# Orders at three stage changes, w_ada a place ahead, and early splits moved off Pool

## The chip, the cores and the metric

One core of a Trainium2 chip runs the whole block in one launch. The metric is device time in microseconds, the median of the runs shown.

## The reference

One transformer-like block in float32 on x of 1024 tokens by 1024 channels:

```
mod = silu(c) @ w_ada + b_ada            # 6 x 1024 columns: shift, scale, gate, twice
h  = rmsnorm(x) * (1 + scale_m) + shift_m
z  = h @ w_in                            # q, k, v, forget logits, pool, conv, 3 x 1024 gate logits
y  = sum over 3 branches of sigmoid(gate) * (branch @ w_branch part)
x  = x + gate_m * rmsnorm(y @ w_out)
h2 = rmsnorm(x) * (1 + scale_f) + shift_f
out = x + gate_f * rmsnorm(relu(h2 @ w_ff1)**2 @ w_ff2)
```

The branches are causal attention with forget gates (8 heads), causal pooling means, and a gated short convolution.

## The kernel before, in words

Every large product is made of three float32r matmuls: each operand is split into a high part (a copy rounded to float32r, `hi`) and a low part (`lo` = operand - hi), and hi·hi, hi·lo and lo·hi are summed in PSUM. A split is two instructions: `split` (L112) and `fsplit` (L686) put the copy on ACT and the subtraction on DVE; `pool_split` (L117) puts both on Pool (GpSimd); `early_split` (L126) the copy on ACT, ahead of its turn, and the subtraction on Pool; `mixed_split` (L121) the copy on Pool and the subtraction on DVE.

The work goes in stages on one core, from memory through SBUF:

1. Start (L137 to L390). x comes in halves of four token tiles. `norm_half` (L258) squares each on ACT, makes 1/rms and scales each tile; the string `XE` (L34) says for each of eight tiles which engine scales it (G Pool, A ACT, V DVE). Column by column k, two 128x1024 tiles of w_ada are loaded on SP's queue and reduced against silu(c) by one DVE instruction each (`ada`, L229), `am` (L317) is made from them, the tile is transposed on TensorE, ACT makes `h` and the high part of `hT`, DVE the low part (L288). w_va (128x264 per k, L322) is split on Pool; three weight tiles of the conv branch (`U_LOADS`, L312) are loaded and split there too. The raw buffers of w_va are two.
2. q, k, v, attention, pooling and conv, with projections woven in (to about 410 us).
3. Gates. Four gate tiles by plain projection (`gate`, L607: sigmoid on ACT, then a store through Pool's queue to DRAM), then ten pairs of gate tiles in a seven-product scheme (`gate_pair`, L807), for which the four `hT` quadrants are combined to `G1` to `G4` first (L764 to L793), each split by `fsplit`. In the pairs, `more_ada` (L617) is called four times a pair: it loads one more w_ada tile and reduces it at once. These tiles, raw weights and sums share eight buffers, tag `M`. After pair 8, `mod_rows` makes the rows for the later norms.
4. Branch projections and merge; then the output projection, token tile by token tile (`out_tile`, L1003): x is loaded again, the result scaled and added, and x2 stored to DRAM on SP's queue (L1030). `h2T_pair` (L1036) transposes two tiles of h2 into the operands `B11`, `B12`, `B21`, `B22`; for the first two pairs it also stores them through Pool's queue (L1054) from three buffers `h2t`.
5. w_ff1, again in a seven-product scheme over 16 pairs: `first_two` (two products X and Y, no transformed operand), `last_five` (with `T1` to `T4`). The first `first_two(0)` stands ahead of the last `h2T_pair(3)` in the code; four more follow. squared relu results go to DRAM through Pool's queue.
6. w_ff2 (L1205 on), seven products of eight steps each; operands come by `load_u`, `load_b` and `parts`. The first two are traced under `tc.high_priority()`, and then the relu of the last w_ff1 result, `X_last` (L1278), whose PSUM bank the new stage takes over. Last, the final norm and the stores.

What sets the order: engines work their instructions in order, each with its own stream, and SP's and Pool's DMA queues are in order too. The framework's scheduler fills these streams from the traced code: of the instructions that its own estimate of times holds ready, the one traced first goes first; `tc.high_priority()` puts a block ahead of that, and `tc.issue_after(i)` puts every instruction of the block that runs on i's engine behind i in that engine's stream (other engines are not bound by it). A tile that is asked for waits until its buffer is free; an instruction waits at the head of its stream.

Of the kernel before, what the change touches and what calls it, by code (L numbers as in the profile page):

```python
# [11 lines left out]
AF = mybir.ActivationFunctionType  # L12
ALU = mybir.AluOpType

P = 128
# [6 lines left out]
HALF = 512  # L22
# [8 lines left out]

EARLY = 5

XE = "GGAAGAVA"  # L34

PLAN = {
    0: "h1", 2: "q1", 4: "k1", 14: "p0 q2 m0", 16: "b1", 22: "p1 q3 m1",
# [16 lines left out]
def kernel(  # L54
# [17 lines left out]
    nc = tc.nc  # L72
# [37 lines left out]
    def f32(ap):  # L110
        return ap.bitcast(F32)
# [2 lines left out]
        A.activation(hi, src, AF.Copy)  # L114
        V.tensor_tensor(out=lo, in0=src, in1=f32(hi), op=ALU.subtract)

    def pool_split(hi, lo, src):  # L117
        G.tensor_scalar(hi, src, 1.0, 0.0, op0=ALU.mult, op1=ALU.add)
        G.tensor_tensor(out=lo, in0=src, in1=f32(hi), op=ALU.subtract)

    def mixed_split(hi, lo, src):  # L121
        G.tensor_scalar(hi, src, 1.0, 0.0, op0=ALU.mult, op1=ALU.add)
        with tc.high_priority():
            V.tensor_tensor(out=lo, in0=src, in1=f32(hi), op=ALU.subtract)

    def early_split(hi, lo, src):  # L126
        with tc.high_priority():
            A.activation(hi, src, AF.Copy)
        G.tensor_tensor(out=lo, in0=src, in1=f32(hi), op=ALU.subtract)

    def load_w(src, parts=split, tag=None, rtag=None):
        raw = sb(rtag or tag or "raw", name="wr")
# [93 lines left out]

    cbs = [cb]

    def ada(i, tag):  # L229
        w = sb(tag, name="wa")  # L230
        nc.sync.dma_start(w, w_ada[i])
        V.tensor_tensor_reduce(out=w, in0=w, in1=cbs[0], scale=1.0, scalar=colt[:, C_BADA + i:C_BADA + i + 1],  # L232
                               op0=ALU.mult, op1=ALU.add, accum_out=modc[:, i:i + 1])

# [74 lines left out]
    xv_i, xa_i = norm_half(0)  # L309

    uw = [None] * 3
    U_LOADS = {0: (0, 11, pool_split, None), 2: (1, 10, early_split, None), 4: (2, 12, early_split, "B")}  # L312
    for k in range(KT):
        with tc.issue_after(xv_i.ins):
            ada(8 + k, "B")
            ada(k, "B")
        V.scalar_tensor_tensor(out=am[:, k:k + 1], in0=modc[:, 8 + k:9 + k], scalar=1.0,  # L317
                               in1=colt[:, C_GMPRE + k:C_GMPRE + k + 1], op0=ALU.add, op1=ALU.mult)
        if k % 2 == 0:
            wvA[k // 2] = sb("M", F32R, (P, 2, 2, VA), name="wva")  # L320
        raw = sb("raw", name="wvr", shape=(P, VA))
        nc.sync.dma_start(raw, w_va[k])  # L322
        pool_split(wvA[k // 2][:, k % 2, 0, :], wvA[k // 2][:, k % 2, 1, :], raw)
        hT_half(0, k)
        if k in U_LOADS:
            with tc.issue_after(xa_i.ins):
                i, m, parts, tag = U_LOADS[k]
                uw[i] = load_w(w_in[m], parts, tag, "B")

    def load_wvb(k2):  # L330
        raw = sb("raw", name="wvr", shape=(P, 2, VB))
        nc.sync.dma_start(raw, w_vb[k2])
        wvB[k2] = sb("M", F32R, (P, 2, 2, VB), name="wvb")
        (split if k2 % 2 else pool_split)(wvB[k2][:, :, 0, :], wvB[k2][:, :, 1, :], raw)

    for i in (0, 2):
        load_x(4 + i)
# [266 lines left out]
        return [lambda: proj(10 + 3 * m, ev_h), lambda: proj(11 + 3 * m, ev_c), last]  # L604


    def gate(j, b):  # L607
        def ev(pp, hf, cs):
            sg_ = sb("G", shape=(P, HALF), name="sig")
            A.activation(sg_, pp, AF.Sigmoid)  # L610
            nc.gpsimd.dma_start(sig_d[b][j][hf], sg_)

        proj(16 + 3 * j + b, ev)

    ada_rest = list(range(16, 48))

    def more_ada(n):  # L617
        for _ in range(n):
            if ada_rest:
                ada(ada_rest.pop(0), "M")  # L620

    conv1, pools = [], []

# [60 lines left out]
    K1, K2 = slice(0, HALF), slice(HALF, D)  # L684

    def fsplit(hi, lo, src):  # L686
        A.activation(hi, src, AF.Copy)  # L687
        V.tensor_tensor(out=lo, in0=src, in1=f32(hi), op=ALU.subtract)  # L688

    def load_half(src):  # L690
        r = tile_of(mpool, "M", 8, name="w1r")
# [21 lines left out]
    def product(p, o, c0, bs, start):  # L713
        for k in range(4):
            ks = slice(c0 + k * P, c0 + (k + 1) * P)
            a, b = o[:, 0, ks], o[:, 1, ks]
            r0, r1 = bs[k]
            T.matmul(p, a, r0, start=(start and k == 0), stop=False, skip_group_check=True)
            T.matmul(p, a, r1, start=False, stop=False, skip_group_check=True)
            T.matmul(p, b, r0, start=False, stop=(k == 3), skip_group_check=True)  # L720

    def two_parts(t):
        return t[:, 0, :], t[:, 1, :]
# [6 lines left out]
    HT = (P, 2, HALF)  # L730
    for b in (1, 2):
        for j in (0, 1):
            gate(j, b)
    close_pool("big")
    qpool = open_pool("qpool")

# [28 lines left out]
    for k in range(4):  # L765
        if k % 2 == 0:
            t1p, t2p = (tile_of(mpool, "M", 8, HT, name=n) for n in ("t1p", "t2p"))
        t1, t2 = t1p[:, k % 2, :], t2p[:, k % 2, :]
        t2s.append(t2)

        tsum(t1, f32(q12[k][0]), f32(q11[k][0]), ALU.subtract)
        tsum(t2, f32(q12[k][1]), f32(q11[k][1]), ALU.subtract)
        tsum(t1, t1, t2, ALU.add)

        tsum(t2, f32(q22[k][0]), t1, ALU.subtract)
        tsum(t2, t2, f32(q22[k][1]), ALU.add)
        fsplit(G2[k][:, 0, :], G2[k][:, 1, :], t2)
        fsplit(G1[k][:, 0, :], G1[k][:, 1, :], t1)

    def more_sums():  # L780
        for k in range(4):
# [16 lines left out]
    def sig_out(b, j, hf, src):  # L798
        r = g_sig()
        A.activation(r, src, AF.Sigmoid)  # L800
        nc.gpsimd.dma_start(sig_d[b][j][hf], r)

    def snap_of(tile, p):
        A.activation(tile, p, AF.Copy)
# [76 lines left out]
    for i, (b, j) in enumerate(todo):  # L881
        if i == 1:
            cb2 = sb("M", name="cb2")
            nc.sync.dma_start(cb2, cb_d.broadcast_to([P, D]))
            cbs[0] = cb2
        last = i == len(todo) - 1
        gate_pair(b, j, *nxt_op, i == 0, to_branches if last else None)
        if not last:
            nxt_op = gate_op(*todo[i + 1])
        if i == 8:  # L890
            mod_rows()
    close_pool("qpool")

# [109 lines left out]
    def out_tile(t):  # L1003
# [20 lines left out]
        for n in range(2):  # L1024
# [2 lines left out]
            V.scalar_tensor_tensor(out=y, in0=pss[n], scalar=rsy[:, t:t + 1], in1=gmb[:, ns],  # L1027
                                   op0=ALU.mult, op1=ALU.mult)
            V.tensor_tensor(out=xt[:, ns], in0=xt[:, ns], in1=y, op=ALU.add)
        nc.sync.dma_start(x2_d[t], xt)  # L1030
        A.activation(yt, xt, AF.Square, accum_out=ss2[:, t:t + 1])
        rstd(ss2[:, t:t + 1], rs2[:, t:t + 1])
        V.tensor_scalar(yt, xt, rs2[:, t:t + 1], None, op0=ALU.mult)
# [75 lines left out]
    def plus(p, s_):  # L1109
        V.tensor_tensor(out=s_, in0=p, in1=s_, op=ALU.add)  # L1110
        return s_

    def first_two(j):
        r1, o = prep_a(j)
        X = fbank("X", 5)
        product(X, o, 0, [two_parts(t) for t in B11], True)
        s1 = snap(X)
        Y = fbank("Y", 1)
        product(Y, o, HALF, [two_parts(t) for t in B21], True)
        c = plus(Y, s1)  # L1120
        if j < EARLY:

# [33 lines left out]
        tag = z_x.pop(0)  # L1156
        return fbank(tag, z_n[tag])

    h2T_pair(3, pairs[3], t_bank, lambda: tile_of(fpool, "ur", 3, (P, HALF)))
    begun += [first_two(j) for j in range(1, EARLY)]  # L1160
    T1, T2, T3, T4 = ([tile_of(tpool, n, 4, HT, F32R) for _ in range(4)] for n in ("t1", "t2", "t3", "t4"))

# [65 lines left out]
    def step(bank, kk, uop, wop, ts=range(4), first=False, last=False):  # L1228
        for k in range(2):
            for t in ts:  # L1230
# [4 lines left out]
                T.matmul(bank[t], a, r1, start=False, stop=False, skip_group_check=True)  # L1235
                T.matmul(bank[t], b, r0, start=False, stop=(last and k == 1), skip_group_check=True)  # L1236

    def parts(u, w):
        uh, ul = g2("uh", 2, F32R), g2("ul", 2, F32R)
        fsplit(uh, ul, u)  # L1240
        wh, wl = g2("wh", 2, F32R), g2("wl", 2, F32R)
        fsplit(wh, wl, w)
        return (uh, ul), (wh, wl)

    def banks(tag):
# [25 lines left out]
    early = []  # L1271
    for kk in range(2):
        pace[0] = None
        with tc.high_priority():
            early.append(first_parts(kk))

    c, r = (g2("sn", 12, shape=(P, HALF)) for _ in range(2))
    A.activation(c, X_last, AF.Relu)  # L1278
    V.scalar_tensor_tensor(out=r, in0=c, scalar=0.0, in1=c, op0=ALU.max, op1=ALU.mult)
    nc.gpsimd.dma_start(u_d[1][(NJ - 1) // 2][:, (NJ - 1) % 2, :], r)  # L1280
    close_pool("fps")
# [152 lines left out]
```

## Time and profile before

| | us |
|---|---|
| median of 3 runs | 1467.77 (1467.15 to 1468.43) |
| profiled execution, its own time | 1467.91 |
| its span, first to last instruction | 1466.2 |
| TensorE matmul busy | 1414.1 (96%) |
| DVE, ACT, POOL busy | 1015.9, 624.5, 234.0 |

Times in the rows are microseconds from the start of the span. PE is TensorE's matmuls, PEld its weight loads, DVE VectorE, ACT ScalarE, POOL GpSimd, SPq the queue on which SyncE issues DMAs. A matmul row's length is modelled with its pipeline; idle time between matmuls is the time lost.

### The profile page before, as it was taken

The numbers are of one execution on the slowest core, as the hardware profiler recorded it, in microseconds if no ns is written. First come the engines' busy times: TensorE is split into PE (matmuls) and PEld (weight loads), VectorE is DVE, ScalarE is ACT, GpSimd is POOL, SyncE is SP. The second block draws the span as 40 slices with busy tenths as digits, with TensorE's granted clock in tenths as the row PEclk, the third lists the DMA queues.
The fourth block names the chain that finished last, engine by engine and source line by source line (L and its number), as shares of the span: only waits on it lengthen the run. The fifth ranks groups of instructions, "written<-read, shape, count | busy, mean of one in ns | idle before, by whom it ended". The sixth has DMA issues, their size and how long they took to land. (4 is left out here: it accounts for less than half of the span.)

```text
span 1466.2 us, 18470 instructions
## 1 busy us (share of the span) xinstructions
PE 1414.1 (96%) x6599; PEld 1155.3 (79%) x6599; DVE 1015.9 (69%) x1892; ACT 624.5 (43%) x1100; POOL 234.0 (16%) x332
## 2 busy tenths in 40 slices
PE   6999999999999999999999899999999899999997
PEld 4898888887877877778788678888888788888875
DVE  7753589797969975378756697555553447998587
ACT  4522356465844333342155653332232343434343
POOL 6401334332311101100011011111111000000230
PEclk9999999999999999999999999999999999999999
DMA  7511111212225866377523534333323786535333
GB/s 268 209 44 45 43 44 44 88 44 70 68 94 184 297 215 202 117 263 259 172 92 127 205 136 138 115 115 108 108 87 103 272 318 195 167 114 173 115 108 136
DMA packets 64854, 209.02 MB, mean 143 GB/s; under 512 B 8874, under 2 KB 9978, under 8 KB 64763
## 3 DMA queue, kind: packets, MB, share of 16 engines
q1 hardware_dynamic: 54970, 176.37, 35.8%
q0 software_dynamic: 9792, 31.47, 5.6%
q8 instruction: 52, 0.85, 0.2%
q14 instruction: 40, 0.32, 0.1%
HBM read 163.73 MB, written 44.09 MB: 142 GB/s over the span
## 5 line engine op out<-in xcount | busy, mean ns | idle before, releaser
L687 ACT ACTIVATE uh<-u 128x1024 fp32r<-128x1024 f32 x56 | 59.3, 1060 | 162.1 <-PE X L1235 72.2
L688 DVE TENSOR_TENSOR ul<-u,uh 128x1024 fp32r<-128x1024 f32 x56 | 69.1, 1235 | 78.6 <-ACT uh L687 78.6
L352 PE MATMUL ps_mm<-hT,whi 128*128 128x512 f32 x272 | 108.5, 399 | 0.0
L354 PE MATMUL ps_mm<-hT,wlo 128*128 128x512 f32 x272 | 108.3, 398 | 0.0
L353 PE MATMUL ps_mm<-hT,whi 128*128 128x512 f32 x272 | 108.1, 397 | 0.0
L688 DVE TENSOR_TENSOR op<-s,op 128x1024 fp32r<-128x1024 f32 x52 | 63.5, 1221 | 59.2 <-ACT op L687 59.0
L1234 PE MATMUL X<-wh,uh 128*128 128x512 f32 x256 | 99.9, 392 | 3.5 <-ACT wh L687 3.5
L1235 PE MATMUL X<-wl,uh 128*128 128x512 f32 x256 | 101.0, 394 | 2.3 <-DVE wl L688 2.3
L1236 PE MATMUL X<-wh,ul 128*128 128x512 f32 x256 | 100.4, 392 | 0.0
L232 DVE CUSTOM_DVE_ANT_0 wa<-wa,cb,colt 128x1024 f32<-128x1024 f32 x48 | 62.7, 1316 | 19.0 <-DMA wa<-in_w_ada_dram 19.0
L1235 PE MATMUL Y<-wl,uh 128*128 128x512 f32 x192 | 75.2, 392 | 0.0
L1236 PE MATMUL Y<-wh,ul 128*128 128x512 f32 x192 | 74.8, 389 | 0.0
L687 ACT ACTIVATE op<-s 128x1024 fp32r<-128x1024 f32 x52 | 54.8, 1056 | 41.8 <-PE Y L720 22.0
L1234 PE MATMUL Y<-wh,uh 128*128 128x512 f32 x192 | 72.1, 389 | 0.0
L1102 POOL DMA_DIRECT2D u_d<-ur x58 | 31.3, 540 | 250.3 <-DVE ur L1101 250.3
L688 DVE TENSOR_TENSOR wl<-w2r,wh 128x1024 fp32r<-128x1024 f32 x56 | 69.2, 1237 | 0.2 <-ACT wh L687 0.2
L1358 POOL TENSOR_TENSOR yl<-sn,gfb 128x512 f32<-128x512 f32 x12 | 24.3, 2037 | 260.8 <-DVE ul L688 244.8
L516 POOL TENSOR_SCALAR prob<-prob,sm 128x128 f32<-128x128 f32 (+3 forms) x64 | 51.4, 803 | 88.1 <-DVE sm L515 81.8
L543 PE MATMUL ps_av<-PT,vS 128*128 128x256 f32 x320 | 60.1, 294 | 2.4 <-ACT PT L114 1.3
L687 ACT ACTIVATE wh<-w2r 128x1024 fp32r<-128x1024 f32 x56 | 58.7, 1050 | 5.9 <-DVE w2r L1333 1.8
L543 PEld LDWEIGHTS ps_av<-PT,vS 128*128 128x128 f32 x320 | 48.2, 188 | 15.2 <-ACT PT L114 7.1
L1235 PEld LDWEIGHTS X<-wl,uh 128*128 128x128 f32 x256 | 48.5, 189 | 14.4 <-DVE wl L688 4.4
(446 smaller groups left out, 4060.7 us busy)
## 6 DMA issues: line engine op xcount, KB each, us to landing
w2r<-in_w_ff_dram SPq DMA_DIRECT2D x64, 512.0 KB, 3.7
wa<-in_w_ada_dram SPq DMA_DIRECT2D x48, 512.0 KB, 4.9
w1r<-in_w_ff_dram SPq DMA_DIRECT2D x37, 512.0 KB, 3.9
u<-u_d SPq DMA_DIRECT2D x32, 512.0 KB, 4.6
u_d<-ur POOLq DMA_DIRECT2D x63, 256.0 KB, 2.3
sig_d<-sig POOLq DMA_DIRECT2D x48, 256.0 KB, 3.2
sig<-sig_d SPq DMA_DIRECT2D x48, 256.0 KB, 3.9
wr<-in_w_in_dram SPq DMA_DIRECT2D x20, 512.0 KB, 3.6
```

Source lines behind the costliest of these rows:

```text
L232: V.tensor_tensor_reduce(out=w, in0=w, in1=cbs[0], scale=1.0, scalar=colt[:, C_BADA + i:C_BADA + i + 1], op0=ALU.mult, op1=ALU.add, accum_ ...
L352: T.matmul(p, a, r0, start=(i == 0), stop=False)
L353: T.matmul(p, a, r1, start=False, stop=False)
L354: T.matmul(p, b, r0, start=False, stop=(i == n - 1))
L516: G.tensor_scalar(pr_[:, :L], pr_[:, :L], sm, 0.0, op0=ALU.mult, op1=ALU.add)
L543: last_pe[0] = T.matmul(av[:, :256], st, PT[:, pp, offs[jj]:offs[jj] + 256], start=(j == 0 and pp == 0), stop=(j == nj - 1 and pp == 1))
L687: A.activation(hi, src, AF.Copy)
L688: V.tensor_tensor(out=lo, in0=src, in1=f32(hi), op=ALU.subtract)
L1102: nc.gpsimd.dma_start(u_d[q][j // 2][:, j % 2, :], r)
L1234: T.matmul(bank[t], a, r0, start=(first and k == 0), stop=False, skip_group_check=True)
L1235: T.matmul(bank[t], a, r1, start=False, stop=False, skip_group_check=True)
L1236: T.matmul(bank[t], b, r0, start=False, stop=(last and k == 1), skip_group_check=True)
```

## The change

`XE` names no Pool tile, and all early splits use `split`; those of w_va are put behind the last ACT scaling of the half. `more_ada` reduces the tile asked for in the call before and asks for the next one; a last call stands ahead of `mod_rows`. The second half of the last plain gate tile stays in PSUM (`kept`), and its sigmoid is put behind the last `G1` split on ACT, with a tile of the next pool. x2 is stored through Pool's queue. The last `h2T_pair` is put behind the first `first_two`'s Y product on TensorE. The first two operand pairs of w_ff2 lose their high priority, and the relu of `X_last` is put behind the last of their splits on ACT.

```diff
-XE = "GGAAGAVA"
+XE = "AVAVAAVA"
...
-    def pool_split(hi, lo, src):
-        G.tensor_scalar(hi, src, 1.0, 0.0, op0=ALU.mult, op1=ALU.add)
-        G.tensor_tensor(out=lo, in0=src, in1=f32(hi), op=ALU.subtract)
...
-    def early_split(hi, lo, src):
-        with tc.high_priority():
-            A.activation(hi, src, AF.Copy)
-        G.tensor_tensor(out=lo, in0=src, in1=f32(hi), op=ALU.subtract)
...
-    def ada(i, tag):
-        w = sb(tag, name="wa")
-        nc.sync.dma_start(w, w_ada[i])
+    def ada(i, tag, w=None):
+        if w is None:
+            w = sb(tag, name="wa")
+            nc.sync.dma_start(w, w_ada[i])
...
-    U_LOADS = {0: (0, 11, pool_split, None), 2: (1, 10, early_split, None), 4: (2, 12, early_split, "B")}
+    U_LOADS = {0: (0, 11, split, None), 2: (1, 10, split, None), 4: (2, 12, split, "B")}
...
-        pool_split(wvA[k // 2][:, k % 2, 0, :], wvA[k // 2][:, k % 2, 1, :], raw)
+        with tc.issue_after(xa_i.ins):
+            split(wvA[k // 2][:, k % 2, 0, :], wvA[k // 2][:, k % 2, 1, :], raw)
...
-        (split if k2 % 2 else pool_split)(wvB[k2][:, :, 0, :], wvB[k2][:, :, 1, :], raw)
+        split(wvB[k2][:, :, 0, :], wvB[k2][:, :, 1, :], raw)
...
-    def gate(j, b):
+    kept = []
+
+    def gate(j, b, keep=False):
         def ev(pp, hf, cs):
+            if keep and hf:
+                kept.append(pp)
+                return
...
+    asked = []
+
     def more_ada(n):
         for _ in range(n):
+            if asked:
+                ada(*asked.pop(0))
             if ada_rest:
-                ada(ada_rest.pop(0), "M")
+                w = sb("M", name="wa")
+                i = ada_rest.pop(0)
+                nc.sync.dma_start(w, w_ada[i])
+                asked.append((i, "M", w))
...
-            gate(j, b)
+            gate(j, b, (b, j) == (2, 1))
...
-        fsplit(G1[k][:, 0, :], G1[k][:, 1, :], t1)
+        split_i = fsplit(G1[k][:, 0, :], G1[k][:, 1, :], t1)
...
+    with tc.issue_after(split_i.ins):
+        sig_out(2, 1, 1, kept[0])
...
         if i == 8:
+            more_ada(1)
             mod_rows()
...
-        nc.sync.dma_start(x2_d[t], xt)
+        nc.gpsimd.dma_start(x2_d[t], xt)
...
-            T.matmul(p, b, r0, start=False, stop=(k == 3), skip_group_check=True)
+            i = T.matmul(p, b, r0, start=False, stop=(k == 3), skip_group_check=True)
+        return i
...
-        product(Y, o, HALF, [two_parts(t) for t in B21], True)
+        prod_i[0] = product(Y, o, HALF, [two_parts(t) for t in B21], True)
...
-    h2T_pair(3, pairs[3], t_bank, lambda: tile_of(fpool, "ur", 3, (P, HALF)))
+    with tc.issue_after(prod_i[0].ins):
+        h2T_pair(3, pairs[3], t_bank, lambda: tile_of(fpool, "ur", 3, (P, HALF)))
...
-        fsplit(wh, wl, w)
+        split_w[0] = fsplit(wh, wl, w)
...
-        with tc.high_priority():
-            early.append(first_parts(kk))
+        early.append(first_parts(kk))
...
-    A.activation(c, X_last, AF.Relu)
+    with tc.issue_after(split_w[0].ins):
+        A.activation(c, X_last, AF.Relu)
```

## Rows read from the trace of the kernel before

**Rows 1.** The page, busy time by engine.

```profile
PE 1414.1 (96%) x6599; PEld 1155.3 (79%) x6599; DVE 1015.9 (69%) x1892; ACT 624.5 (43%) x1100; POOL 234.0 (16%) x332
```

**Rows 2.** Waits of TensorE by releaser: us in total, times, longest.

```profile
PE Z L1042 <- ACT h2t L1052: 3.3, 1, 3.3
PE ps_mm L300 <- DVE hT L288: 3.2, 2, 1.8
PE ps_mm L718 <- DVE sn L726: 2.9, 2, 1.8
```

**Rows 3.** Six stretches: length, then busy per engine, granted clock, DMA share, GB/s.

```profile
11.00:44.00 33.00, 23.48 (x112) 17.54 (x113) 28.01 (x36) 10.90 (x14) 25.06 (x20) 1.00 0.75 277
427.00:455.00 28.00, 22.88 (x93) 16.55 (x92) 26.09 (x40) 18.04 (x28) 1.08 (x2) 1.00 0.39 131
545.00:575.00 30.00, 27.13 (x109) 21.08 (x108) 20.83 (x29) 9.94 (x15) 2.83 (x6) 0.94 0.53 171
818.00:836.00 18.00, 12.79 (x60) 10.21 (x59) 11.70 (x24) 12.80 (x25) 0.00 (x0) 0.81 0.69 253
823.90:830.70 6.80, 4.98 (x15) 4.03 (x16) 6.36 (x11) 5.30 (x10) 0.00 (x0) 0.50 0.45 154
855.00:879.00 24.00, 21.99 (x88) 17.18 (x87) 23.47 (x37) 11.80 (x18) 2.44 (x5) 0.93 0.51 176
1142.00:1152.00 10.00, 5.57 (x17) 3.83 (x15) 5.33 (x5) 4.38 (x5) 0.94 (x2) 0.83 0.43 150
```

**Rows 4.** Groups of DVE, 9 to 56 us: busy us, mean ns, idle before.

```profile
L232 DVE CUSTOM_DVE_ANT_0 wa<-wa,cb,colt 128x1024 f32<-128x1024 f32 x16 | 22.1, 1388 | 1.1 <-DMA wa<-in_w_ada_dram 1.1
L288 DVE TENSOR_TENSOR hT<-h,hT 128x512 fp32r<-128x512 f32 x8 | 11.8, 1476 | 5.7 <-ACT hT L287 5.5
L317 DVE SCALAR_TENSOR_TENSOR am<-modc,colt 128x1 f32<-128x1 f32 x8 | 4.1, 514 | 0.1
```

**Rows 5.** Timeline of DVE near 567 us: start, length, what, idle before.

```profile
567.08 1.28 DVE L232 CUSTOM_DVE_ANT_0 wa<-wa,cb,colt 128x1024 f32<-128x1024 f32 x1 [3.31 <-DMA wa<-in_w_ada_dram]
```

**Rows 6.** Groups of DVE, 60 to 90 us.

```profile
L288 DVE TENSOR_TENSOR hT<-h,hT 128x512 fp32r<-128x512 f32 x8 | 5.2, 687 | 5.9 <-ACT hT L287 5.9
...
L272 DVE TENSOR_SCALAR x<-x,rs 128x1024 f32<-128x1024 f32 x1 | 0.7, 746 | 0.0
```

**Rows 7.** Timeline of DVE and PE in the gate pairs.

```profile
539.78 0.15 DVE L667 SCALAR_TENSOR_TENSOR af<-modc,colt 128x1 f32<-128x1 f32 x1
539.85 1.22 DVE L688 TENSOR_TENSOR op<-w1r,op 128x1024 fp32r<-128x1024 f32 x1
...
551.30 0.40 PE L718 MATMUL ps_mm<-hT,op 128*128 128x512 f32 x1
...
574.52 0.49 PE L718 MATMUL ps_mm<-hT,op 128*128 128x512 f32 x1
```

**Rows 8.** The page's costliest groups, one of DVE's.

```profile
L688 DVE TENSOR_TENSOR wl<-w2r,wh 128x1024 fp32r<-128x1024 f32 x56 | 69.2, 1237 | 0.2 <-ACT wh L687 0.2
```

**Rows 9.** Timeline of ACT and DVE at the first gate pair.

```profile
427.34 0.60 ACT L610 ACTIVATE sig<-ps_mm 128x512 f32<-128x512 f32 x1 [4.97 <-PE ps_mm L354]
...
428.91 1.23 DVE L688 TENSOR_TENSOR op<-w1r,op 128x1024 fp32r<-128x1024 f32 x1 [11.93 <-ACT op L687]
```

**Rows 10.** Timeline of SP's queue and ACT at the end of the output projection.

```profile
811.79 0.33 SPq L1030 DMA_DIRECT2D x_d<-x  x1
...
818.25 0.60 ACT L1020 ACTIVATE yt<-ps_s 128x512 f32<-128x512 f32 x1 [4.55 <-PE ps_s L1019]
...
825.36 2.94 ACT L687 ACTIVATE op<-w1r 128x1024 fp32r<-128x1024 f32 x3
```

**Rows 11.** Timeline of ACT at the start of the last GEMM.

```profile
1142.89 0.60 ACT L1278 ACTIVATE sn<-X 128x512 f32<-128x512 f32 x1 [7.65 <-PE X L720]
```

**Rows 12.** Timeline of Pool's and SP's queues, output projection, pair 0.

```profile
761.27 0.54 POOL L1054 DMA_DIRECT2D h_d<-h2t  x1 [125.21 <-ACT ru L240]
...
764.69 0.33 SPq L1030 DMA_DIRECT2D x_d<-x  x1
```

More of the change, by code (lines that the diff above doesn't have):

```diff
@@ L686, in fsplit @@
     def fsplit(hi, lo, src):
-        A.activation(hi, src, AF.Copy)
+        i = A.activation(hi, src, AF.Copy)
         V.tensor_tensor(out=lo, in0=src, in1=f32(hi), op=ALU.subtract)
+        return i
     def load_half(src):
@@ L719, in product @@
             T.matmul(p, a, r1, start=False, stop=False, skip_group_check=True)
-            T.matmul(p, b, r0, start=False, stop=(k == 3), skip_group_check=True)
+            i = T.matmul(p, b, r0, start=False, stop=(k == 3), skip_group_check=True)
+        return i
     def two_parts(t):
@@ L1111, in plus @@
         return s_
+    prod_i = [None]
     def first_two(j):
@@ L1236, in step @@
                 T.matmul(bank[t], b, r0, start=False, stop=(last and k == 1), skip_group_check=True)
+    split_w = [None]
     def parts(u, w):
```

## The prediction

> **What bounds the kernel now.** I read the page's busy times first. TensorE is busy 1414.1 us, 96% of the span [rows 1]: whatever the other engines do counts only where TensorE stands still or runs at the lower clock. The waits of TensorE by releaser say where that is [rows 2]: at a change of stage (for `h2t`, at the end of the output projection), in the ramp for `hT`, and in the gate stage for DVE's sums. Six stretches then tell what each place costs [rows 3]; length less PE busy is the idle time.
>
> - 11 to 44 us, the ramp: 33.00 - 23.48 = 9.5 us idle. DVE is busy 28.01 and POOL 25.06, so neither PE nor memory sets the pace (DMA share 0.75).
> - 427 to 455, first gate pair: 5.1 us idle, DVE busy 26.09 of 28.
> - 545 to 575, two later gate pairs: 2.9 us idle. The granted clock is 0.94, so 30 x 0.06 = 1.8 us of full speed are lost as well.
> - 818 to 836, end of the output projection: 5.2 us idle; from 823.9 to 830.7 the granted clock is 0.50 (1.2 GHz), and half of the 4.98 busy us, 2.5, is lost.
> - 855 to 879, the transformed h2 operands: 2.0 us idle, 24 x 0.07 = 1.7 us of clock, DVE busy 23.47 of 24.
> - 1142 to 1152, start of the last GEMM: 4.4 us idle, 10 x 0.17 = 1.7 us of clock.
>
> The clock's part comes on top of the idle. All six: 29.1 idle + 7.7 of clock = 37 us, the most that ordering could return.
>
> **The change, part by part** (signs: minus is faster).
>
> *Early splits (ramp).* Pool's splits go to ACT and DVE, as do its two x scalings of the first half. What DVE gives and takes: while Pool works, DVE's operations are long. The 16 column sums of w_ada take 1388 ns against 1.28 us later [rows 4, 5]: 16 x 0.11 = 1.7 us. The 8 `hT` subtractions take 1476 against 687 ns with Pool quiet [rows 4, 6]: 6.3 us. The 8 one-column `am` operations take 514 ns, where the same form takes 0.15 us in the gate stage [rows 4, 7]: 2.9 us. Together 10.9 us come off DVE. Added: eight `wva` lows of 264 columns, estimated 0.42 us from the 512- and 1024-column subtractions (687 and 1237 ns [rows 6, 8]), 3.4 us; three `wlo`, 3.7 us; two x scalings of 0.75 [rows 6], 1.5 us. Sum 8.6. Net 2.3 us shorter, and the new lows can fill DVE's 6.8 us of waits in the ramp (1.1 for DMA, 5.7 before `hT`) [rows 4]. Ends: 8.6 slower if Pool isn't what lengthened DVE; 9.1 faster if all waits fill. I take -4.0, net plus a quarter of the holes, since most of that wait is for ACT's `hT`, which still comes after DVE's own `am`. The raw buffers are freed by DVE now, and SP's w_ada loads queue behind those; ACT has room (10.90 of 33). The second half's x scaling and the two `wvb` splits come when TensorE has v and conv work queued: nothing.
>
> *w_ada asked a place ahead (gate stage).* Each DMA is issued a call before its sum. At 567.08 DVE had stood 3.31 us for one [rows 5], and behind it in DVE's order came the split and the sum that TensorE waited 2.9 us for (`sn` L726 [rows 2]). The sums keep their 1.28 us, the loads their count; each tile is held one call longer. I take the 2.9 us and 1.6 of the 1.8 clock: -4.5 (ends 0 and -4.7). The one flush ahead of the modulation rows may still wait: +1.6, half the 3.31.
>
> *Last gate's second sigmoid kept back.* ACT stood 4.97 us for the last projection's PSUM at 427.34, with the next pair's split behind it; DVE then began at 428.91 after 11.93 us idle [rows 9]. With the sigmoid behind the last G1 split, ACT's nine splits start about 5 us earlier, and so does DVE, which is 93% busy through this stage. Idle 5.1; I take -4.5 (ends -2.0, as DVE stays nearly full, and -5.1). The kept bank is one of three `mm`; the next pair needs one more. The late sigmoid and its Pool store feed loads of a later stage: nothing.
>
> *x2 through Pool's queue, transposes behind the first product.* SP issued an x2 store at 811.79, which waits for DVE, and w_ff1's first loads stand behind it in SP's order; ACT then stood 4.55 us before 818.25, but the first `op` split ran at 825.36, after the pair-2 evacuations [rows 10]. With the store off SP, the loads can go as soon as their buffers and the x load before them allow, and the split fits into ACT's idle time. The first two products, 24 matmuls, then fill the wait that the pair-3 transposes make (3.3 us for `h2t` alone [rows 2]). Gain 5.2 idle + 2.5 clock = 7.7. Late next is DVE: at 855 to 879 it is 98% busy, and TensorE comes 7.7 us earlier while DVE, which had 18 - 11.70 = 6.3 us idle from 818 to 836, can use some 5.5 of these once it has the pair-3 inputs sooner. So 2.2 come back there: -5.5 (ends 0 and -7.7). Eight stores of 512 KB join Pool's queue, beside the `h_d` stores only; their price stands in a rival.
>
> *Relu of the last X behind the first w2 splits.* ACT stood 7.65 us for X at 1142.89, then ran relu and four splits in a row [rows 11]: the inputs could be split in that wait. Idle 4.4 + clock 1.7 = 6.1. The relu now frees its bank behind the splits, up to 1.0 late: -5.1 (ends -3.0, if DVE's lows stay behind its last sums, and -6.1).
>
> **Sum.** -4.0 + 1.6 - 4.5 - 4.5 - 5.5 - 5.1 = -22.0 us. It is made against the profiled execution, 1467.91 us (span 1466.2 and 1.7 around it), 0.14 above the median of the three runs: 1446 us.
>
> **The rivals.**
>
> *Pool's queue becomes the wait.* In pair 0 the first `h_d` store went at 761.27, the x2 store of tile 2 at 764.69 [rows 12]. If the x2 store stands first in Pool's order, the h_d stores wait 3.4 us for it; the three h2t buffers fill, ACT stands and TensorE's transposes wait for PSUM. Two pairs: 2 x (3.4 + about 1.7 of clock) = 10.2: 1456.2. For it: the code puts the store ahead. Against: the scheduler goes by readiness. The `h_d` store at 761.27 took 0.54 us to issue, so the rows give no more than that for a store. The Trainium skill ("SBUF — State Buffer", section "A bandwidth-pool intuition that's wrong (but worth ruling out)") speaks against this part: a DMA from Pool's queue that takes about 620 ns alone takes about 3100 beside a DVE copy, since its descriptors can't be written while DVE holds the port that the two share; by that an estimate of 2.5 us would come on top in each of the two pairs, and this rival would end at 1461.
>
> *The first product's split stays late.* If `op` still runs at 825.4, TensorE waits for it in place of the transposes; the 5.5 fall away: 1451.5. For: the change orders TensorE only, not ACT. Against: ACT's 4.55 us hole.
>
> *DVE is too full in the ramp.* If Pool wasn't what slowed DVE, +8.6 in place of -4.0: 1458.6. Against: 687 ns with Pool quiet.
>
> *The orders bind nothing.* If the edges leave ACT's splits where the scheduler had them, the 4.5 and 5.1 of the kept sigmoid and the relu are lost: 1455.6.
>
> *Slower: too few M tiles in the gate stage.* w_ada holds a tile of eight one call longer, and SP is in order, so weight loads queue behind it. A pair begins at 551.30 and the next at 574.52, with four calls in it: 5.8 us a call. The next pair's `op` was split at 539.85 (1.22 us) and first used at 551.30 [rows 7]: 10.2 us of slack. That is the point: one call's delay costs nothing, two (11.6) cost 1.4 us in each of 8 pairs, with 1.7 of clock each: 25, and the 4.5 gain is lost: 1446 + 4.5 + 25 = 1475.5. Against: five live tiles a pair in eight.
>
> **How the numbers follow.** Forecast 0.50, late split 0.14, Pool's queue 0.12, edges bind nothing 0.10, full DVE 0.08, M tiles 0.06. Low end: every part at its good end, -9.1 - 4.7 - 5.1 - 7.7 - 6.1 = -32.7, hardly all at once; 1436 leaves a little of that out. High end: the full-DVE rival's 1458.6 with a little room; 1460 takes in all rivals but the last. About 0.2% (2.9 us) is what a measurement can tell from no change: under 1464.8 counts as faster. Faster 0.88, same 0.05, slower 0.07 (the last rival and a pile-up of others).
>
> **What would show it.** Right: DVE's `hT` subtractions near 690 ns in the ramp and TensorE steady some 4 us sooner; no `sn` L726 wait; ACT's `op` split before 424; X and Y products of the first w_ff1 tile ahead of the Z transposes with no long PE gap and no 0.50 clock there; `uh` split before 1142 on the old time scale. A longer PE wait near 860 to 875 would be the part given back. Wrong: PE waits on `op` splits in each gate pair, POOL `h_d` stores waiting for DVE's x, or DVE's ramp ending later than now.

## The result, and the profile after

The changed kernel takes 1450.24 us (1449.89 to 1453.03, 4 runs) against 1467.46 (1465.95 to 1468.43, 4 runs) for the kernel before: ratio 0.9882, 95% interval 0.9867 to 0.9898. The forecast was 1446.0, the range 1436 to 1460. The profiled execution took 1449.98 us, its span 1448.1.

The page's busy times by engine:

```profile
PE 1406.4 (97%) x6599; PEld 1151.8 (80%) x6599; DVE 1011.2 (70%) x1907; ACT 629.7 (43%) x1112; POOL 202.2 (14%) x313
```

TensorE's work is the same 6599 matmuls, now busy 7.7 us less [rows 1]. About 3.3 us of that is the clock: 8.7 us of its busy time ran at half clock, in place of 15.2. The rest is not split up here. The waits of TensorE by releaser (us in total, times, longest):

```profile
PE X L725 <- ACT op L693: 4.8, 1, 4.8
PE ps_pt L275 <- ACT h L277: 3.9, 2, 3.5
PE ps_pt L275 <- ACT x L267: 3.6, 2, 3.3
...
PE ps_mm L725 <- DVE sn L734: 3.2, 2, 1.9
```

Of the three waits in [rows 2], the one for `h2t` is gone and one for the first w_ff1 split, `op`, stands in its place and is longer; the one for DVE's `sn` in the gate stage is there still; the one for `hT` has shrunk to 0.3. The two waits `ps_pt` for ACT stand at the ramp's very start. The stretches that answer to [rows 3], each at its place on the new time scale (length, then busy per engine, granted clock, DMA share, GB/s):

```profile
11.00:44.00 33.00, 27.53 (x152) 22.64 (x153) 29.35 (x57) 16.45 (x26) 0.00 (x0) 1.00 0.88 335
417.00:445.00 28.00, 25.35 (x107) 19.36 (x106) 25.80 (x40) 16.44 (x27) 1.08 (x2) 1.00 0.43 140
536.00:566.00 30.00, 28.67 (x125) 23.16 (x124) 19.12 (x28) 10.77 (x15) 2.69 (x5) 1.00 0.55 185
812.00:830.00 18.00, 13.17 (x56) 10.28 (x55) 12.91 (x22) 12.85 (x24) 1.07 (x2) 0.81 0.51 179
815.40:822.20 6.80, 5.26 (x12) 3.67 (x13) 6.05 (x8) 4.26 (x6) 0.00 (x0) 0.50 0.48 162
843.00:867.00 24.00, 23.93 (x103) 19.00 (x102) 24.00 (x39) 12.84 (x21) 2.70 (x5) 1.00 0.42 150
1127.00:1137.00 10.00, 9.31 (x41) 7.24 (x40) 6.53 (x7) 1.66 (x2) 1.62 (x3) 1.00 0.58 210
```

Read against [rows 3], three places gain: the ramp's idle time falls from 9.5 to 5.5 us, the start of the last GEMM has 0.7 us idle and full clock, and the stretch of the transposed operands has none. The first gate pair still has 2.7 us idle. The end of the output projection looks as before: 4.8 us idle, and 6.8 us at half clock.

Where the time went is seen best when the same work is compared: the n-th matmul of both traces, start against start, in one profiled execution of each kernel.

| place, time in the changed kernel | the changed kernel is ahead by | step | the step's term |
|---|---|---|---|
| 400, ramp over | 6.5 us | 6.5 | 4.0 |
| 440, first gate pair | 9.8 | 3.3 | 4.5 |
| 600, gate pairs | 8.8 | -1.0 | 4.5, less 1.6 |
| 700 to 805 | 9.5 | 0.7 | 0 |
| 832 to 860, transposed operands | 8.6 | -0.9 | (7.7) |
| 886 to 1120, w_ff1 | 12.1 | 3.5 | (-2.2), together 5.5 |
| 1145, last GEMM started | 17.6 | 5.5 | 5.1 |
| end of span | 18.05 | 0.4 | 0 |

### The profile page after: what moved, and what is told of

It is laid out like the page before. It is cut to its first block, busy times and chain, and to the rows that moved or that the text cites. A ratio compares the mean times of both kernels' runs of the same rounds, so it can differ in the third digit from the quotient of the medians.

```text
span 1448.1 us, 18454 instructions
## 1 busy us (share of the span) xinstructions
PE 1406.4 (97%) x6599; PEld 1151.8 (80%) x6599; DVE 1011.2 (70%) x1907; ACT 629.7 (43%) x1112; POOL 202.2 (14%) x313
## 4 chain that ended last, share of the span: by engine, by line
PE 73%; DVE 10%; issue 8%; DMA 6%; ACT 2%; POOL 1%; SPq 0%; DVEq 0%; POOLq 0%; ACTq 0%
PE ps_mm L347 5%; PE ps_mm L346 5%; PE ps_mm L345 5%; PE X L727 4%; PE X L1251 4%; PE X L1250 4%; PE X L726 4%; PE X L725 4%; PE X L1252 4%; PE Y L1251 3%; PE Y L1250 3%; PE Y L1252 3%; DMA wa<-in_w_ada_dram 3%; PE ps_av L536 2%; PE Z L727 2%
## 5 line engine op out<-in xcount | busy, mean ns | idle before, releaser
L536 PEld LDWEIGHTS ps_av<-PT,vS 128*128 128x128 f32 x320 | 48.1, 188 | 15.2 <-ACT PT L114 7.1
L347 PEld LDWEIGHTS ps_mm<-hT,wlo 128*128 128x128 f32 x272 | 51.2, 188 | 9.8
```

The source lines that it names most:

```text
L347: T.matmul(p, b, r0, start=False, stop=(i == n - 1))
L536: last_pe[0] = T.matmul(av[:, :256], st, PT[:, pp, offs[jj]:offs[jj] + 256], start=(j == 0 and pp == 0), stop=(j == nj - 1 and pp == 1))
```

## The experiments

Unless said otherwise each run is the changed kernel with the edit shown, and its time is held against 1450.24 us. "Ahead" and "behind" are by the n-th matmul, as in the table. The runs of one kernel lie up to some 5 us apart (1449.4 to 1454.64 for one below), so where two medians differ by less than some 3 us, the place by place comparison of one profiled execution each is what tells more.

**The ramp.** Pool gets its early splits and x scalings back.

```diff
-XE = "AVAVAAVA"
+XE = "GGAAGAVA"
...
-            split(wvA[k // 2][:, k % 2, 0, :], wvA[k // 2][:, k % 2, 1, :], raw)
+            pool_split(wvA[k // 2][:, k % 2, 0, :], wvA[k // 2][:, k % 2, 1, :], raw)
```

> The changed kernel with the early splits and x scalings given back to Pool; all else as changed. Theory (Pool lengthens DVE's operations in the ramp, and the new DVE work costs less than it gives back): 1456.8 us, +6.6 over 1450.2; DVE's hT subtractions in the ramp average about 1.48 us again instead of about 0.7, and TensorE's matmuls are shifted by +6.5 from the attention on. Rival (the ramp's gain came from the earlier start and the new order, not from Pool): the subtractions grow but the time stays within 2 us of 1450.

Measured: 1458.02 us (1455.41 to 1458.87), 7.8 slower. It is 6.7 us behind at 400 us, and DVE's `hT` subtractions are back at 1477 ns. The second run adds Pool work that nothing needs:

```diff
+    scratch = misc[:, 256:640]
+    G.memset(scratch, 0.0)
+    for _ in range(26):
+        G.tensor_tensor(out=scratch, in0=scratch, in1=scratch, op=ALU.add)
```

> The changed kernel with 26 additions of 128x384 on Pool put into the ramp, on a scratch region that nothing reads there; no split is given back. Theory (Pool's two-input work alone lengthens DVE's): DVE's hT subtractions in the ramp go from about 0.7 us to over 1.2 mean, w_ada sums from 1.28 to about 1.4, and the time to 1456 to 1462. Rival (what lengthened DVE was its waiting for data, not Pool): the durations stay and the time stays at 1450 within 1.

Measured: 1461.9 us (1461.62 to 1462.28), 11.7 slower, most of it by 45 us (10.4 us behind there, 12.0 at the end). The groups of DVE from 9 to 56 us (busy us, mean ns, idle before), first of the changed kernel, which answers to [rows 4]:

```profile
L224 DVE CUSTOM_DVE_ANT_0 wa<-wa,cb,colt 128x1024 f32<-128x1024 f32 x16 | 20.4, 1283 | 2.5 <-DMA wa<-in_w_ada_dram 2.4
L280 DVE TENSOR_TENSOR hT<-h,hT 128x512 fp32r<-128x512 f32 x8 | 5.5, 692 | 1.3 <-ACT hT L279 1.2
L115 DVE TENSOR_TENSOR wlo<-wr,whi 128x1024 fp32r<-128x1024 f32 x3 | 3.7, 1224 | 1.0 <-ACT whi L114 1.0
L115 DVE TENSOR_TENSOR wva<-wvr,wva 128x264 fp32r<-128x264 f32 x8 | 3.4, 430 | 0.0
...
L309 DVE SCALAR_TENSOR_TENSOR am<-modc,colt 128x1 f32<-128x1 f32 x8 | 1.3, 159 | 0.0
```

Then of the run with idle Pool work:

```profile
L224 DVE CUSTOM_DVE_ANT_0 wa<-wa,cb,colt 128x1024 f32<-128x1024 f32 x16 | 24.8, 1560 | 1.3 <-DMA wa<-in_w_ada_dram 1.3
L280 DVE TENSOR_TENSOR hT<-h,hT 128x512 fp32r<-128x512 f32 x7 | 6.7, 951 | 0.4 <-ACT hT L279 0.3
...
L313 DVE SCALAR_TENSOR_TENSOR am<-modc,colt 128x1 f32<-128x1 f32 x7 | 2.9, 418 | 0.0
```

The splits are on ACT and DVE in both, so what differs in the second fence has only Pool's presence to answer for. Its means mix two kinds of instruction, since Pool's additions end at 38.52 us. Pool's timeline in this run, then DVE's:

```profile
8.90 29.62 POOL L305 TENSOR_TENSOR misc<-misc 128x384 f32<-128x384 f32 x22
```

```profile
36.53 1.30 DVE L280 TENSOR_TENSOR hT<-h,hT 128x512 fp32r<-128x512 f32 x1
...
41.25 0.69 DVE L280 TENSOR_TENSOR hT<-h,hT 128x512 fp32r<-128x512 f32 x1
```

While the additions run, each `hT` and each `am` is 0.61 us longer, each `wa` 0.56 (1.84 for 1.28) and each `wlo` 0.62; after them all are back at the lengths of the changed kernel. That is also why the mean of `hT`, 951 ns, missed the 1.2 us expected, while that of `wa`, 1560, came out above the 1.4. That Pool slows DVE is shown, and not only argued from the two kernels.

**w_ada, asked for a place ahead.** The first run takes this one part back.

```diff
-            if asked:
-                ada(*asked.pop(0))
             if ada_rest:
-                w = sb("M", name="wa")
-                i = ada_rest.pop(0)
-                nc.sync.dma_start(w, w_ada[i])
-                asked.append((i, "M", w))
+                ada(ada_rest.pop(0), "M")
```

> The changed kernel without asking for w_ada a place ahead in the gate stage. Theory now (the load is issued when the buffer of the last sum comes free, wherever it stands in the code): 1450 within 1.5, DVE's waits for w_ada again some 18 to 22 us in total between 440 and 600. Rival (the prediction's: asking ahead takes the waits off): 1454 or more, with DVE's waits grown by over 5 us.

Measured: 1447.34 us (1446.32 to 1447.52), 2.9 faster than the changed kernel; against the kernel before 0.986 (0.9843 to 0.9876). It is the fastest of all. DVE's waits for w_ada from 440 to 600 us, of the kernel before, of the changed kernel and of this run in turn (us in total, times, longest):

```profile
DVE wa L232 <- DMA wa<-in_w_ada_dram: 17.9, 11, 3.3
```

```profile
DVE wa L224 <- DMA wa<-in_w_ada_dram: 22.0, 14, 3.3
```

```profile
DVE wa L224 <- DMA wa<-in_w_ada_dram: 18.6, 11, 3.4
```

The change made them longer. SP's queue runs ahead of DVE with or without it: from the issue of a load to its sum there are 7.1 us on average in the kernel before, 6.9 in the changed one and 7.1 here (32 loads each). In the changed kernel SP's own waits ahead of these loads, from 440 to 600 us, are 99.1 us, and 98.1 of them are for DVE: 52.7, in 15 waits, for the end of an earlier sum, 21.7 for a split. A load can't leave until DVE is that far, so one wait of DVE can lead straight to the next. The timeline of DVE, then that of TensorE, in the changed kernel (start, length, what, idle before and its releaser):

```profile
518.11 1.28 DVE L224 CUSTOM_DVE_ANT_0 wa<-wa,cb,colt 128x1024 f32<-128x1024 f32 x1 [3.31 <-DMA wa<-in_w_ada_dram]
...
520.46 0.68 DVE L734 TENSOR_TENSOR sn<-ps_mm,sn 128x512 f32<-128x512 f32 x1
```

```profile
521.20 0.50 PE L725 MATMUL ps_mm<-g,oc 128*128 128x512 f32 x1 [1.88 <-DVE sn L734]
```

This is the same chain as at 567.08 in [rows 5], with the same 3.31 us, 46 us sooner. After it the granted clock falls (0.96 from 500 to 545 us, 1.8 us of full speed), which it doesn't in the run without the asking ahead (1.00). That run gets ahead by 2.5 us between 440 and 700, but the fall of the clock is not the reason by itself. Two runs further down ask ahead too and keep a clock of 1.00 there, the one with a held M buffer and the first with a split in M tiles; from 440 to 600 us TensorE then stands idle for 5.8 and 5.4 us, against 4.0 in the changed kernel and 3.5 without asking ahead, and at 805 us they are level with the changed kernel (0.3 and 0.7 us behind).

The next run moves one of the four sums of a pair behind the sum that TensorE waited for:

```diff
...
-        more_ada(n_ada)
         product(X, o34, 0, g3, False)
         if not hook:
-            tsum(p5, X, p5, ALU.add)
+            t_i = tsum(p5, X, p5, ALU.add)
+            with tc.issue_after(t_i.ins):
+                more_ada(n_ada)
```

> The changed kernel with the third w_ada sum of each gate pair put behind the sum p5 on DVE instead of ahead of it. Theory (what TensorE waits for at 521 and 563 is DVE standing at a w_ada sum with the split and p5 behind it): these two waits (1.9 and 1.3 us) and the low clock after the first go, 1446 to 1447. Rival (the late sum frees its buffer later, so the next load is late and the wait shows at the next sum): 1450 within 1, with TensorE waits of the same total at another sum.

Measured: 1451.02 us (1450.9 to 1453.88), no gain. The low clock is gone (1.00 from 500 to 545 us), as the theory had it, but the wait goes to another of the four sums, for which DVE stands 3.28 us at 498.04, with a split and TensorE's sum behind it:

```profile
502.83 0.50 PE L725 MATMUL ps_mm<-g,oc 128*128 128x512 f32 x1 [2.28 <-DVE sn L734]
```

The last run on this part was to make M buffers scarcer.

```diff
+        if i == 1:
+            held = sb("M", name="held")
+            G.memset(held, 0.0)
...
+            G.memset(held, 1.0)
```

> The changed kernel with one of the eight M buffers held (two Pool memsets of a tile, one before the second gate pair and one after the ninth, so that it is taken in between). Theory (the buffers, not the place in the code, set when a w_ada load starts): DVE's waits for w_ada in the gate stage, 22.0 us in the changed kernel, grow past 30 us, and the kernel is 3 us slower or more, 1453 or above. Rival (the loads start when SP's queue comes to them, and a buffer is always free): 1449.5 to 1451.5, and the waits stay near 22 us.

Measured: 1449.81 us (1449.0 to 1450.68), DVE's waits 24.3 us. It is inconclusive, since it didn't do what it was for; Pool's timeline has both memsets at the start of the stage:

```profile
423.01 0.96 POOL L900 MEMSET held<- 128x1024 f32 x1 [0.62 <-DVE g L694]
424.02 0.95 POOL L906 MEMSET held<- 128x1024 f32 x1
```

Nothing tied the second to a later time, so the buffer was held for 2 us. Whether the number of buffers or the choice of the buffer ties a load to an earlier sum stays open.

**The kept sigmoid.**

```diff
-            gate(j, b, (b, j) == (2, 1))
+            gate(j, b)
...
-    with tc.issue_after(split_i.ins):
-        sig_out(2, 1, 1, kept[0])
```

> The changed kernel with the last plain gate tile's second sigmoid evacuated at once again, as before the change. Theory (ACT's nine splits waited behind that sigmoid): the stalls of 1.63 and 0.29 us at the first gate pair's start come back, and the two traces put this place at 3.3 us, so about 1453.5 us. The prediction's own term of 4.5 gives 1454.7. Rival (the gain there came from the ramp's earlier finish, not from the sigmoid): no change, 1450.2.

Measured: 1456.35 us (1454.95 to 1457.43), 6.1 slower. ACT's timeline shows the cause (the nine splits follow, TensorE's wait is under it):

```profile
420.98 0.60 ACT L608 ACTIVATE sig<-ps_mm 128x512 f32<-128x512 f32 x1 [4.99 <-PE ps_mm L347]
421.47 1.05 ACT L693 ACTIVATE op<-w1r 128x1024 fp32r<-128x1024 f32 x1
```

```profile
422.57 0.50 PE L725 MATMUL ps_mm<-hT,op 128*128 128x512 f32 x1 [1.63 <-ACT op L693]
```

In the changed kernel that first split ran at 415.76. The theory holds; its size is off: by 440 us this run is 4.1 behind where 3.3 was expected, for it also has a stretch of lower clock (0.83 from 420 to 430). Another 3.1 us go between 440 and 700, where the gate pairs' stalls fall differently.

**The relu.**

```diff
-        early.append(first_parts(kk))
+        with tc.high_priority():
+            early.append(first_parts(kk))
...
-    with tc.issue_after(split_w[0].ins):
-        A.activation(c, X_last, AF.Relu)
+    A.activation(c, X_last, AF.Relu)
```

> The changed kernel with the relu of the last w_ff1 result ahead of the first w_ff2 splits on ACT again, those two operand pairs under high priority as before. Theory (the relu held up the splits): the 3.5 us wait for ACT's wh and the 0.9 for DVE's wl at the start of the last GEMM come back with the clock's fall, 5.5 us between the two traces, so about 1455.7 us. Rival (DVE's low parts stay behind its last sums whatever ACT does, and the splits gain little): at most 2 us, under 1452.3.

Measured: 1457.47 us (1455.07 to 1459.15), 7.2 slower; the profiled execution, its fastest, is 5.1 slower, and by the matmuls the place itself costs 5.5. ACT's timeline, then TensorE's:

```profile
1130.25 0.60 ACT L1296 ACTIVATE sn<-X 128x512 f32<-128x512 f32 x1 [7.65 <-PE X L727]
1130.74 1.99 ACT L693 ACTIVATE uh<-u 128x1024 fp32r<-128x1024 f32 x2
1132.63 1.99 ACT L693 ACTIVATE wh<-w2r 128x1024 fp32r<-128x1024 f32 x2
```

```profile
1133.73 0.73 PE L1250 MATMUL X<-wh,uh 128*128 128x512 f32 x2 [3.52 <-ACT wh L693]
1135.37 0.80 PE L1251 MATMUL X<-wl,uh 128*128 128x512 f32 x1 [0.90 <-DVE wl L694]
```

The four splits run one behind the other after the 7.65 us wait, as in [rows 11]. In the changed kernel they ran in that wait, between 1123.0 and 1128.4.

**x2's queue, and the transposes.** Two runs, each with one part back.

```diff
-        nc.gpsimd.dma_start(x2_d[t], xt)
+        nc.sync.dma_start(x2_d[t], xt)
```

> The changed kernel with the x2 stores on SP's queue again; the other engines' orders stay as they are. Theory (in the changed kernel ACT's first op split stands behind the evacuations of the pair before in ACT's order, so the earlier load buys nothing): 1449.7 to 1450.8 us, and TensorE waits as long for op as before, 4.8 us. Rival (the prediction's: the load of w_ff1's first tile sets the split): the split runs some 3 to 5 us later, 1453 to 1455.

```diff
-    with tc.issue_after(prod_i[0].ins):
+    if True:
         h2T_pair(3, pairs[3], t_bank, lambda: tile_of(fpool, "ur", 3, (P, HALF)))
```

> The changed kernel without the edge that puts the last pair's transposes behind the first tile's X and Y products on TensorE. Theory (the edge made what this stage gained, since it keeps the transposes' evacuations from standing between the stage's last products): about 2.6 us slower, 1452.8, with a PE wait for h2t of about 3 us as in the kernel before. Rival (what TensorE gains from the edge it loses in its wait for the late op split): no change, 1449.7 to 1450.8.

Measured: 1451.57 us (1449.4 to 1454.64) with x2 on SP's queue, 1.3 slower and 0.8 above the theory's upper end; but from 805 to 886 us its distance to the changed kernel stays the same (1.6 and 1.4 us behind, both from the gate stage). w_ff1's loads are issued 8.65 us later by the two clocks, some 7 when those 1.6 are taken off, and TensorE's wait is the same 4.79; SP's queue in the changed kernel, then in this run, and TensorE's timeline in this run:

```profile
795.62 2.56 SPq L699 DMA_DIRECT2D w1r<-in_w_ff_dram  x5
```

```profile
804.27 3.01 SPq L699 DMA_DIRECT2D w1r<-in_w_ff_dram  x5
```

```profile
818.55 0.80 PE L725 MATMUL X<-b,op 128*128 128x512 f32 x1 [4.79 <-ACT op L693]
```

Why the earlier load bought nothing is on ACT's timeline of the changed kernel, which answers to [rows 10]:

```profile
808.71 0.60 ACT L1033 ACTIVATE yt<-ps_s 128x512 f32<-128x512 f32 x1 [4.55 <-PE ps_s L1032]
...
815.81 3.88 ACT L693 ACTIVATE op<-w1r 128x1024 fp32r<-128x1024 f32 x4
```

ACT still stands 4.55 us for the last token tile with the split far behind in its order.

Without the edge: 1452.64 us (1451.57 to 1454.34), 2.4 slower, which alone is within what the medians can tell apart; by the matmuls 1.3 of it is lost in this stage. TensorE's timeline:

```profile
815.38 0.48 PE L1055 MATMUL Z<-ident,yt 128*128 128x128 f32 x1 [3.29 <-ACT h2t L1065]
...
864.07 0.50 PE L725 MATMUL X<-t,op 128*128 128x512 f32 x1 [1.69 <-ACT op L693]
```

Up to 860 us this run is even 0.7 us ahead of the changed one: the edge gave nothing at its own place, a wait of 3.29 for one of 4.79. It pays at 864, where without it ACT stands 3.36 us for an X bank at 862.47 with a split behind it; with it the scheduler has that split, at 862.00, ahead of the bank's read. ACT's timeline without the edge, then in the changed kernel:

```profile
862.47 0.60 ACT L1163 ACTIVATE sn<-X 128x512 f32<-128x512 f32 x1 [3.36 <-PE X L727]
862.97 1.05 ACT L693 ACTIVATE op<-s 128x1024 fp32r<-128x1024 f32 x1
```

```profile
862.00 1.06 ACT L693 ACTIVATE op<-s 128x1024 fp32r<-128x1024 f32 x1 [4.17 <-DVE s L705]
```

By 886 us the run is 1.2 behind.

**The split that stayed late.** It is put into two M tiles and traced under high priority, and so lies in ACT's idle time. A second run takes the asking ahead away too.

```diff
...
+        if j == 0:
+            hi, lo = (tile_of(mpool, "M", 8, dtype=F32R, name=n) for n in ("oph", "opl"))
+            with tc.high_priority():
+                fsplit(hi, lo, r)
+            return r, Two(hi, lo)
```

> The changed kernel with the first w_ff1 tile's split put into two M tiles in place of one op tile and traced under high priority, so that in ACT's order it stands in ACT's idle time before the last token tile's PSUM read, ahead of the evacuations of the pair before. Theory (this split's late place is what kept the output projection's gain from coming): the 4.8 us wait of the product X for ACT's op goes, and with it the stretch at half clock from 815 to 822 us (3.4 us of full speed); 5 to 8 us faster than the changed kernel, 1442 to 1445. Rival (the wait moves on to the transposes' evacuations or to DVE, which is nearly full from 830 to 890 us): under 2 us faster, 1448.5 or more.

> As the run before this one, and w_ada not asked for a place ahead (one undone part of the change). Theory: both gains add, 2.9 us below the run before this one, 1439 to 1442. Rival (the 2.9 us of the undone part came from where the stalls happened to fall, and don't add): the same time as the run before this one, within 1.5 us.

Measured: 1451.53 us (1449.38 to 1453.54, 5 runs) and 1449.88 (1447.72 to 1451.38). Neither theory held as a time. The second run does get the gate stage's gain (at 805 us it is 3.7 ahead of the changed kernel, where the first is 0.7 behind), but it is 2.5 slower than the run with the asking ahead alone undone (1447.34): there was no gain of the split to add. The first run's split is at 804.73, the 4.8 us wait and the half clock are gone, and at 832 us TensorE is 5.9 us ahead of the changed kernel. At 860 it is 0.9 behind, after a wait of 4.39 us and with a granted clock of 0.89 from 830 to 845: TensorE's timeline, then DVE's, then ACT's:

```profile
834.00 0.50 PE L725 MATMUL Y<-b,op 128*128 128x512 f32 x1 [4.39 <-DVE sn L1135]
```

```profile
832.58 0.76 DVE L1069 TENSOR_TENSOR b<-ur,b 128x256 fp32r<-128x256 f32 x2 [1.71 <-ACT b L1068]
833.26 0.68 DVE L1135 TENSOR_TENSOR sn<-Y,sn 128x512 f32<-128x512 f32 x1
```

```profile
831.68 0.56 ACT L1065 ACTIVATE ur<-Z,modc,af 128x256 f32<-128x256 f32 x1 [2.98 <-DMA u_d<-ur]
```

The only Y bank is emptied by a sum that stands behind two low parts on DVE, these wait for ACT, and ACT for a store that frees one of three `ur` buffers. The last run, on top of the second, puts these two low parts behind that sum:

```diff
...
+    begun.append(first_two(1))
+    with tc.issue_after(sum_i[0].ins):
+        for lo, h, hi in late[2:]:
+            V.tensor_tensor(out=lo, in0=h, in1=hi, op=ALU.subtract)
```

> The run op_m_ada, and on DVE the last two low parts of the last pair's transposed operands put behind the sum that empties the Y bank of the second w_ff1 tile. Theory (in op_m TensorE won 5.9 us by the earlier split and lost 6.2 again because that sum stood behind these low parts, which wait for ACT, which waits 3.0 us for a store to free its buffer): the sum starts some 2.4 us sooner, TensorE's wait of 4.9 us for it falls to 2.5 or less, and with it part of the following stretch at half clock; 1445 to 1447.5 us. Rival (DVE, nearly full from 830 to 890 us, sets the pace there, and a wait comes back further on): 1449 us or more, with a new PE wait between 840 and 890.

Measured: 1449.7 us (1448.98 to 1451.34). The rival has it; TensorE's waits from 805 to 900 us:

```profile
PE Y L720 <- DVE sn L1133: 4.9, 3, 3.1
PE X L720 <- ACT op L688: 2.5, 2, 1.7
```

That wait fell from 4.9 to 1.47 us, and one of 3.08 followed at 836.37, one of 0.82 at 851.30, one of 1.69 at 862.15. This run is ahead of the changed kernel by 3.0 us at 805 (the gate stage's gain), by 9.5 at 832 and by 0.7 at 886: the whole lead of 6.5 is given back, and 2.3 more. From 830 to 890 us its clock is 1.00 and TensorE is busy 53.81 of 60, so this is waiting alone. In the changed kernel DVE is busy 58.14 of the same 60 us and TensorE 59.93; in the three runs DVE is busy 56.61, 57.71 and 56.20. The reading that DVE and ACT set the pace of this stage, and that an earlier TensorE only waits there, fits all three runs but is not shown by them: DVE still had 2.3 to 3.8 us idle, and in the first run its wait came by way of ACT and a store. What is shown is that the lead was lost each time.

## Why the prediction was right, and where it was not

The direction, the size and the range held: 17.2 us came where 22.0 were forecast. The single terms held less well, and that their sum came this near is in part luck: by the runs that undo them, w_ada and the output projection missed by 5.4 and 4.4 us, while the ramp gave 2.7 more than forecast and 3.2 came that no single part accounts for.

**Early splits: right in mechanism, too small.** The durations came out as worked out: `hT` at 692 ns for the 687 taken, `am` at 159 for 0.15 us, `wva` at 430 for 0.42 and `wlo` at 1224. The term is 6.5 us by the traces and 6.7 by the run that undoes it, for 4.0. DVE's timeline has the stretch from the first w_ada sum to the last `hT`; of the changed kernel, then the last of the kernel before, whose first sum is at 12.49:

```profile
12.42 1.28 DVE L224 CUSTOM_DVE_ANT_0 wa<-wa,cb,colt 128x1024 f32<-128x1024 f32 x1
...
48.04 0.69 DVE L280 TENSOR_TENSOR hT<-h,hT 128x512 fp32r<-128x512 f32 x1 [1.23 <-ACT hT L279]
```

```profile
55.28 0.69 DVE L288 TENSOR_TENSOR hT<-h,hT 128x512 fp32r<-128x512 f32 x1 [1.57 <-ACT hT L287]
```

That is 36.3 us in place of 43.5, 7.2 less. 10.8 come off the three groups, for the forecast's 10.9. Of the 8.6 added, the two x scalings' 1.5 stand at 10.11 and 11.63, ahead of the stretch, in time that DVE had free: the step that counted them was wrong. The waits in the groups shown fall from 6.8 us to 4.8, about the quarter that was taken. So 10.8 - 7.1 + 2.0 = 5.7 of the 7.2 are told; the rest was not looked for in single operations.

**w_ada asked ahead: wrong.** The step that failed is "Each DMA is issued a call before its sum", from which the 3.31 us wait was taken to go. SP's stream runs ahead of DVE's anyway, and its loads wait for DVE, for an earlier sum above all; the lead didn't grow (7.1 and 6.9 us), and the part costs 2.9 us where 4.5 less 1.6 was forecast as gain. The slower rival had the sign right but not the price: no 25 us, and no more waits for `op` than before (2.4 us in 2, for 2.8 in 3). Whether a tile held longer is what costs the 2.9, as it says, is not shown. The flush of 1.6 isn't seen as a wait of TensorE.

**Kept sigmoid: right.** 3.3 us by the traces, 4.1 at its place by the run that undoes it, 4.5 taken.

**x2 and the transposes: the rival "the first product's split stays late" held at its place.** The step that failed is "the split fits into ACT's idle time": it could, but nothing in the change moves ACT's order, which the rival said. The wait of 4.79 us and the half clock show it, as does the split at 804.73 once it is put there, and x2's queue is worth nothing that these runs can tell. Yet 2.6 us came, not 0, at 864 to 886, where the prediction had looked for a loss. Some 1.3 of it is the edge's, by an order of ACT that nobody foresaw; the rest is near the 1.7 us of clock that [rows 3] has at 855 to 879 and that the run without the edge doesn't lose either (1.00 from 830 to 890). The general point behind that loss, that the stage can't take in TensorE's lead, is what the last three runs showed, more strongly than forecast: not 2.2 of 7.7 come back but all of it. That DVE's load is the reason fits them and is not shown.

**Relu: right**, 5.5 for 5.1.

**Rivals.** Pool's queue is no wait: the x2 stores took 0.54 us each to issue, and none held back an `h_d` store. The Trainium skill ("SBUF — State Buffer", section "A bandwidth-pool intuition that's wrong (but worth ruling out)") had given some 3100 ns for a Pool DMA beside a DVE copy; here the store at 755.44 us took 0.54 to issue and landed 2.9 us after its start, and the same store from SP's queue, at 756.81 in the run with x2 there, landed after 3.0; so no such delay shows, but DVE worked on subtractions then, not on a copy, and the page's own case was not met. A DVE too full in the ramp and edges that bind nothing are both refuted by the runs that undo those parts.

At their places the undone parts are worth 6.7 (ramp), 4.0 (sigmoid), 5.5 (relu), 1.3 (edge), -0.2 (x2) and -2.5 us (w_ada), 14.8 together of the 18.05 between the spans. The other 3.2 lie where parts meet, mostly in the gate stage, and no run here splits them up. By their medians the six come to some 22 us for 17.2, so no part has an exact price of its own.

## What to carry to other kernels

Before a load is asked for earlier in the code, look at what its issue waits for in its queue; where the queue already ran ahead and waited for an engine, as here, the place in the code bought nothing. An order put on one engine doesn't move the work that it waits for on another: check that engine's own order for what stands ahead. And before a stall is paid for, look at the stage behind it: here the engine next in line was 94 to 97% busy, and the stall was only moved.

## What the hardware showed unasked

Pool work that no one waits for made most of DVE's instructions longer by nearly one amount, whatever their size, for as long as it ran: 0.61 us for 512 columns, 0.61 for one column, 0.56 for a 1024-column sum, 0.62 for a 1024-column subtraction. The means shown for that run hide this, since they also count the instructions after Pool's last addition. The Trainium skill (the same page and section) says of two operations that slow each other that this is "a structural stall, not bandwidth sharing"; the one amount agrees with that, but not all instructions had it: the two x scalings were 0.32 us longer, and the 264-column subtractions were no longer than without (423 and 430 ns). Why these differ is open.

The clock didn't follow the length of a wait: 1.63 us ahead of the first gate pair left it at 1.00 in the kernel before [rows 3] and took it to 0.83 in the run with the sigmoid back; 3.08 us at 836 left it at 1.00. What TensorE did before and after differed each time, and no run here tells what decides.
